# S5 recurrence and C powers moved from GpSimd to VectorE, S5 output steps placed between projections

## The chip, the core and the metric

One core of one Trainium2 chip runs one layer of a decoder for 256 prompt positions and 8 x 4 decode positions. The metric is the device time of one execution in microseconds. The engines are TensorE (PE; PEld is its weight load), VectorE (DVE), ScalarE (ACT), GpSimd (POOL) and SyncE (SP, which issues most loads). Each works through its own queue in order and waits on semaphores for the others.

## The reference, cut to what matters

The layer modulates a normalised input by conditioning vectors (adaLN), projects it to q, k, v, g, a_lr and u, runs gated linear attention (GLA, 4 heads) on the first five and an S5 state space group on u, mixes both through an output projection, and ends with a convolutional feed-forward part. The S5 part, to which the change belongs:

```python
lam_bar = jnp.exp(lam * dt)
b_bar = ((lam_bar - 1) / lam)[..., None] * bmat
bu = jnp.einsum('gpk,blgk->blgp', b_bar, uf.astype(jnp.complex64))
bu = bu.at[:, 0].add(lam_bar * h0)
_, h = lax.associative_scan(combine, (a, bu), axis=1)      # s_t = lam_bar s_(t-1) + bu_t
y = jnp.real(jnp.einsum('gkp,blgp->blgk', cmat, h)) + d_skip.astype(f32) * uf
```

There are 64 groups of 16 channels with 64 complex states each. All of it is float32.

## The kernel before

Activations lie transposed: features on partitions, the 32 decode and 256 prompt positions (288) as columns. A float32 product is made of three matmuls (mm3, L146 to L148): a weight tile `raw` of 128x1024 arrives by DMA, ScalarE rounds it to `wh` (L128), VectorE subtracts to get `wl` (L130, called the weight split), and wh is multiplied with the high and low part of the activation, wl with the high part. The results stand in three PSUM buffers `acc`, which ScalarE or VectorE must evict. Other matmuls: `ada` (L203, the adaLN projections, which run in the gaps of everything up to the feed-forward part), transposes against `ident`, and the small ones of GLA (`gl`) and S5 (`s`).

The input projection takes the 16 blocks of the contraction in K-groups of 2, 2 and 4 (column blocks acc evicted at L614 for the first group, by ScalarE, and at L616 and L618 for the others, by VectorE), and the last 8 of them in `proj2`, called for each of the 32 column blocks when it is wanted: u in 0 to 7, q in 8 to 11, k in 12 to 15, v in 16 to 23, g in 24 to 31. The S5 parameters are prepared beside the first groups: powers of A (`AP`, by `cmul`, L309 to L314), three powers of A times B (`pn`, L356 to L366) which TensorE transposes (L376), and C times the powers of A (`cA`, L394 to L400).

S5 works on blocks of four positions. Each of the eight steps f makes u of four pairs of groups, forms the states' inputs `st` (64 prompt columns and 8 decode columns for each of 2 x 32 rows) with TensorE (L714), and adds to every second column its neighbour times A^4 (`advance`, L684 and L687). Then the odd columns are carried through one after the other: 31 steps of four operations on 128x64 with A^8 (`a8`, L733 to L736), all on GpSimd, with `s5p` copied from the last one (L738). `s5_out(f)` advances the even columns of its f, and TensorE multiplies the states with cA (L895) and u with a local matrix (L891); ScalarE copies the result to `zt` (L898), TensorE transposes it (L901). The attention inside chunks follows a ladder of levels (VectorE L806 to L810, exponentials on ScalarE, TensorE L773 and L787). `dec_states` does the decode states of GLA with TensorE (L972, L984), on states loaded from `sgla` into two pairs of buffers in turn.

The order of the instructions on each engine is set when the program is built: a scheduler takes them by priority and by its own model of the times, with weight loads and splits raised by a fixed amount (AHEAD). `order_after` pins an instruction behind another of the same engine: the advance of an output step behind the eviction of the last g projection (`gadd`).

## Time and profile before

| what | us |
|---|---|
| median of 3 runs | 1459.36 |
| the three runs | 1458.64, 1459.36, 1469.23 |
| the profiled execution, its time | 1467.12 |
| its span (first to last instruction) | 1465.3 |
| TensorE busy in the span | 1408.3 |
| VectorE busy | 908.1 |
| ScalarE busy | 676.8 |
| GpSimd busy | 343.5 |
| mean granted TensorE clock | 0.983 |

The share of busy time is that of the whole span. The stages differ: the first 45 us prepare, the input projection runs to about 200 us, S5, q, k, v, g and attention lie between 200 and 430 us, the output projection follows, and from about 600 us on the feed-forward part fills TensorE. Busy time of TensorE counts a matmul at half clock in full, so the clock has to be read beside it.

### The profile page before, as it was taken

The page shows a single profiled execution, that of the slowest core. Times are in us where ns is not written, and L with a number is a line of the kernel's source. Part 1 is how long each engine was busy: PE and PEld are TensorE (multiplying, and loading weights), DVE is VectorE, ACT ScalarE, POOL GpSimd, SP SyncE. Part 2 cuts the span into 40 slices and gives each one's busy share as a digit, 9 for nine tenths or more (in the row PEclk, how much of TensorE's full clock was granted, in tenths as well). Part 3 has the DMA queues.
Part 4 walks back from the last instruction along what each step waited for, and adds up shares of the span by engine and source line. Part 5 has one row for each costly group of instructions (what it writes and reads, how often), then busy time and mean ns, then how long its engine had stood idle before and what let it go on. Part 6 is the DMA issues. An engine that isn't in the chain of part 4 may idle for free.

```text
span 1465.3 us, 29026 instructions
## 1 busy us (share of the span) xinstructions
PE 1408.3 (96%) x11546; PEld 1301.8 (89%) x11546; DVE 908.1 (62%) x1648; ACT 676.8 (46%) x1132; POOL 343.5 (23%) x616
## 2 busy tenths in 40 slices
...
GB/s 374 333 263 221 342 285 286 285 295 318 148 143 399 281 277 260 278 302 288 166 166 164 168 161 169 161 169 140 191 163 165 166 162 170 160 172 159 138 102 65
DMA packets 88727, 316.96 MB, mean 216 GB/s; under 512 B 10368, under 2 KB 10784, under 8 KB 88592
## 3 DMA queue, kind: packets, MB, share of 16 engines
...
q10 hardware_dynamic: 288, 0.59, 0.1%
...
## 4 chain that ended last, share of the span: by engine, by line
PE 72%; POOL 5%; DMA 1%; DVE 1%; issue 1%; ACT 0%; DVEq 0%; POOLq 0%; ACTq 0%
PE acc L146 22%; PE acc L147 22%; PE acc L148 22%; PE ada L203 2%; POOL st L736 1%; POOL q L733 1%; POOL q L734 1%; POOL st L735 1%; PE s L895 1%; DMA raw<-wadf 0%; PE s L891 0%; DMA o_glap<-S 0%; PE gl L972 0%; PE acc L1184 0%; PE acc L1185 0%
## 5 line engine op out<-in xcount | busy, mean ns | idle before, releaser
L128 ACT CAST wh<-raw 128x1024 fp32r<-128x1024 f32 (+1 forms) x376 | 385.6, 1030 | 565.7 <-PE acc L147 482.8
L130 DVE TENSOR_TENSOR wl<-raw,wh 128x1024 fp32r<-128x1024 f32 (+1 forms) x376 | 458.2, 1221 | 274.6 <-ACT wh L128 261.7
L146 PE MATMUL acc<-hh,wh 128*128 128x288 f32 x1360 | 402.8, 296 | 0.0
L147 PE MATMUL acc<-hl,wh 128*128 128x288 f32 x1360 | 401.1, 295 | 0.0
L148 PE MATMUL acc<-hh,wl 128*128 128x288 f32 x1360 | 399.9, 294 | 0.0
L146 PEld LDWEIGHTS acc<-hh,wh 128*128 128x128 f32 x1360 | 254.7, 187 | 3.6 <-ACT up L1197 1.1
L148 PEld LDWEIGHTS acc<-hh,wl 128*128 128x128 f32 x1360 | 256.1, 188 | 0.0
L147 PEld LDWEIGHTS acc<-hl,wh 128*128 128x128 f32 x1360 | 255.1, 188 | 0.8 <-issue 0.8
L1198 POOL COPY cvo<-up 128x16 f32<-128x16 f32 x88 | 99.6, 1131 | 582.1 <-ACT up L1196 582.1
L147 PE MATMUL acc<-ffhl,wh 128*128 128x288 f32 x704 | 208.1, 296 | 0.0
L148 PE MATMUL acc<-ffhl,wl 128*128 128x288 f32 x704 | 207.6, 295 | 0.0
L146 PE MATMUL acc<-ffhl,wh 128*128 128x288 f32 x704 | 207.0, 296 | 0.5 <-ACT ffhl L1228 0.2
L146 PE MATMUL acc<-h,wh 128*128 128x288 f32 x512 | 158.0, 309 | 2.0 <-DVE PG L618 1.2
L148 PE MATMUL acc<-h,wl 128*128 128x288 f32 x512 | 152.4, 300 | 3.1 <-DVE wl L130 3.1
L147 PE MATMUL acc<-h,wh 128*128 128x288 f32 x512 | 152.9, 299 | 0.9 <-DVE h L483 0.9
L147 PEld LDWEIGHTS acc<-ffhl,wh 128*128 128x128 f32 x704 | 132.7, 188 | 0.1
L146 PEld LDWEIGHTS acc<-ffhl,wh 128*128 128x128 f32 x704 | 131.9, 188 | 0.9 <-ACT ffhl L1228 0.5
L148 PEld LDWEIGHTS acc<-ffhl,wl 128*128 128x128 f32 x704 | 132.0, 188 | 0.0
L1062 DVE SCALAR_TENSOR_TENSOR x<-acc,mod,x 128x256 f32<-128x256 f32 x128 | 61.7, 482 | 101.9 <-PE acc L148 101.7
L146 PEld LDWEIGHTS acc<-h,wh 128*128 128x128 f32 x512 | 97.3, 190 | 24.9 <-issue 10.7
L203 PE MATMUL ada<-raw,cS 128*32 128x512 f32 (+1 forms) x832 | 101.5, 577 | 6.2 <-DMA raw<-wadf 3.7
L148 PEld LDWEIGHTS acc<-h,wl 128*128 128x128 f32 x512 | 96.9, 190 | 4.2 <-DVE wl L130 3.8
...
## 6 DMA issues: line engine op xcount, KB each, us to landing
...
raw<-wadf SPq DMA_DIRECT2D x128, 512.0 KB, 6.8
...
```

What stands on the lines that cost most here:

```text
L128: cast[0] = S.copy(wh, raw)
L130: V.tensor_sub(wl, raw, wh.bitcast(F32))
L146: T.matmul(ps, wh[:, ks], xh(k), start=first, stop=False)
L147: T.matmul(ps, wh[:, ks], xl(k), start=False, stop=False)
L148: tail[0] = T.matmul(ps, wl[:, ks], xh(k), start=False, stop=last).ins
L203: mms.append(lambda c=c, kc=kc_of(blk, j), raw=raw, c0=c0, first=first, last=last: T.matmul(ps[32 * c:32 * c + 32, 0:w], cS[:, kc, :], raw ...
L733: G.tensor_tensor(q1, prev, a8[:, 0], op=ALU.mult)
L734: G.tensor_tensor(q2, prevs, a8[:, 1], op=ALU.mult)
L735: G.tensor_tensor(cur, cur, q1, op=ALU.add)
L736: G.tensor_tensor(cur, cur, q2, op=ALU.add)
L1062: V.scalar_tensor_tensor(x2[:, m, ND:], ps[:, ND:], mod[:, vi, m, 0:1], x2[:, m, ND:], op0=ALU.mult, op1=ALU.add)
L1198: G.tensor_copy(cvo[:, m, 0:16].rearrange("p (b w) -> p b w", w=2), upd[:, :, 4:6])
```

## The change

Five things are changed. The C powers are computed by VectorE instead of GpSimd. The powers A^4, A^8, A^16, A^32 and A^64 (`apr`, `api`) are computed with the S5 parameters in place of `a4` and `a8`. All advances run on VectorE, and the serial recurrence on GpSimd is replaced by `scan` on VectorE: three levels up, three single columns, three levels down, 36 operations, once for the first half of the pair blocks (after f = 3) and once for the second (after f = 7). The output steps stand between the value and first gate projections (`fill(16)` to `fill(25)`), and the last six gate projections among the value transposes, the prompt state and the decode states. The pairs of buffers of the decode states change places.

```diff
@@ -391,13 +391,13 @@
             for n in range(4):
                 ar, ai = bc16(AP[:, n, 0]), bc16(AP[:, n, 1])
                 t1, t2 = tmp512(), tmp512()
-                G.tensor_tensor(t1, cc[:, 0], ar, op=ALU.mult)
-                G.tensor_tensor(t2, cin, ai, op=ALU.mult)
...
+                V.tensor_tensor(t1, cc[:, 0], ar, op=ALU.mult)
+                V.tensor_tensor(t2, cin, ai, op=ALU.mult)
...
@@ -513,6 +513,9 @@
                                      (cst, a["cst"][:, 0:C_ID])):
                         tc.keep_in_program_order(nc.sync.dma_start(dst, src))
 
+        apr = epb.tile([P, 5, 32], F32, name="apr")
+        api = epb.tile([P, 5, 2, 32], F32, name="api")
+
         def s5_rest(w1=w1, w2=w2, w3=w3):
             for o_, sc_ in ((sn, 1.0), (sh_, 0.5)):
                 sin_op = S.activation(o_, thr, AF.Sin, scale=sc_)
@@ -539,6 +542,15 @@
             V.tensor_mul(w2, w3, lam_i)
             V.tensor_sub(w1, w1, w2)
             V.tensor_mul(fi, w1, den)
+
+            for i in range(5):
+                if i == 0:
+                    V.tensor_copy(apr[:, 0], AP[:, 3, 0])
+                    V.tensor_copy(api[:, 0, 1], AP[:, 3, 1])
+                else:
+                    s_r, s_i = apr[:, i - 1], api[:, i - 1, 1]
+                    cmul(apr[:, i], api[:, i, 1], s_r, s_i, s_r, s_i, w1, w2)
+                V.tensor_scalar_mul(api[:, i, 0], api[:, i, 1], -1.0)
 
 
         h2 = [None]
@@ -664,27 +676,31 @@
             V.tensor_sub(l2, l2, l1)
             V.tensor_tensor_scan(cum[:, h], cst[:, C_RST:C_RST + NT], l2, 0.0, op0=ALU.mult, op1=ALU.add)
 
-
-        a4 = epb.tile([P, 2, 2, 32], F32, name="a4")
-        a8 = epb.tile([P, 2, 2, 32], F32, name="a8")
-        for t in (a4, a8):
-            if t is a4:
-                V.tensor_copy(t[:, 0, 0], AP[:, 3, 0])
-                V.tensor_copy(t[:, 1, 1], AP[:, 3, 1])
-            else:
-                cmul(t[:, 0, 0], t[:, 1, 1], AP[:, 3, 0], AP[:, 3, 1], AP[:, 3, 0], AP[:, 3, 1],
-                     t[:, 0, 1], t[:, 1, 0])
-            V.tensor_copy(t[:, 0, 1], t[:, 0, 0])
-            V.tensor_scalar_mul(t[:, 1, 0], t[:, 1, 1], -1.0)
-
-        def advance(eng, dst, src, srcs, fs, n, prev=None):
-            for w_, x in ((0, src), (1, srcs)):
-                q = t2k.tile([P, 512], F32, tag="t2k", name=nm("q"))[:, 0:8 * n].rearrange(
-                    "p (r a c) -> p r a c", r=2, a=4)
-                ins = eng.tensor_tensor(q, x, a4[:, w_, :, fs].unsqueeze(3).to_broadcast([P, 2, 4, n]), op=ALU.mult)
+        def advance(eng, fs, lev, c0, dist, n, prev=None):
+
+            na, back = fs.stop - fs.start, 1 << lev
+
+            def cols(rs, c):
+                return st[:, rs, fs, NB + 1 + c:NB + 2 + c + dist * (n - 1):dist]
+
+            dst = cols(slice(None), c0)
+            for w_, rs in ((0, slice(None)), (1, slice(None, None, -1))):
+                q = t2k.tile([P, 512], F32, tag="t2k", name=nm("q"))
+                q = q[:, 0:2 * na * n].rearrange("p (r a c) -> p r a c", r=2, a=na)
+                tr = (apr[:, lev, fs].unsqueeze(1).to_broadcast([P, 2, na]) if w_ == 0 else api[:, lev, :, fs])
+                ins = eng.tensor_tensor(q, cols(rs, c0 - back), tr.unsqueeze(3).to_broadcast([P, 2, na, n]), op=ALU.mult)
                 if prev is not None and w_ == 0:
                     order_after(ins.ins, prev)
                 eng.tensor_tensor(dst, dst, q, op=ALU.add)
+
+        def scan(eng, fs):
+
+            for lev in (1, 2, 3):
+                advance(eng, fs, lev, (2 << lev) - 1, 2 << lev, NC4 >> (lev + 1))
+            for c in range(31, NC4, 16):
+                advance(eng, fs, 4, c, 1, 1)
+            for lev in (3, 2, 1):
+                advance(eng, fs, lev, (3 << lev) - 1, 2 << lev, (NC4 >> (lev + 1)) - 1)
 
         ut = []
         for f in range(8):
@@ -715,25 +731,17 @@
                 S.copy(st[:, r, 4 * f:4 * f + 4, NB + 1:], pi[:, :, NB:])
                 S.copy(deci[:, r, 4 * f:4 * f + 4], pi[:, :, 0:NB])
             fs = slice(4 * f, 4 * f + 4)
-            advance(V if f == 7 else G, st[:, :, fs, NB + 2::2], st[:, :, fs, NB + 1::2], st[:, ::-1, fs, NB + 1::2], fs, 32)
+            advance(V, fs, 0, 1, 2, NC4 // 2)
+            if f % 4 == 3:
+                scan(V, slice(4 * f - 12, 4 * f + 4))
             step(ada_b, 1)
 
         dt1 = t2k.tile([P, 512], F32, tag="t2k", name="dt1").rearrange("p (r a b) -> p r a b", r=2, a=32)
         for w_, src in ((0, st[:, :, :, 0:NB]), (1, st[:, ::-1, :, 0:NB])):
             for r in range(2):
-                V.tensor_tensor(dt1[:, r], src[:, r], a4[:, w_, r].unsqueeze(2).to_broadcast([P, 32, NB]), op=ALU.mult)
+                V.tensor_tensor(dt1[:, r], src[:, r], (apr[:, 0] if w_ == 0 else api[:, 0, r]).unsqueeze(2).to_broadcast([P, 32, NB]), op=ALU.mult)
             V.tensor_add(deci, deci, dt1)
         G.dma_start(a["o_s5d"], deci)
-        for c in range(3, NC4, 2):
-            prev = st[:, :, :, NB + c - 1]
-            prevs = st[:, ::-1, :, NB + c - 1]
-            cur = st[:, :, :, NB + c + 1]
-            q1 = sml.tile([P, 2, 32], F32, tag="q1", bufs=1, name=nm("q1"))
-            q2 = sml.tile([P, 2, 32], F32, tag="q2", bufs=1, name=nm("q2"))
-            G.tensor_tensor(q1, prev, a8[:, 0], op=ALU.mult)
-            G.tensor_tensor(q2, prevs, a8[:, 1], op=ALU.mult)
-            G.tensor_tensor(cur, cur, q1, op=ALU.add)
-            G.tensor_tensor(cur, cur, q2, op=ALU.add)
         s5p = epb.tile([P, 2, 32], F32, name="s5p")
         G.tensor_copy(s5p, st[:, :, :, NCOL])
         G.dma_start(a["o_s5p"], s5p)
@@ -867,19 +875,13 @@
             S.copy(kFT[blk], pa)
 
 
-        for m in range(16, 24):
-            ps = proj2(m)
-            V.tensor_add(proj_dst(m), ps, proj_dst(m))
-            step(ada_b, 1)
-
         ybuf = []
 
         gadd = [None]
 
         def s5_out(f):
             fs = slice(4 * f, 4 * f + 4)
-            advance(G if f % 2 else V, st[:, :, fs, NB + 3::2], st[:, :, fs, NB + 2:NCOL:2], st[:, ::-1, fs, NB + 2:NCOL:2],
-                    fs, 31, None if f % 2 else gadd[0])
+            advance(V, fs, 0, 2, 2, NC4 // 2 - 1, gadd[0])
             zt = t2k.tile([P, 512], F32, tag="t2k", name=nm("zt"))
             ztv = zt[0:NCOL].rearrange("p (t a j k) -> p a j t k", t=4, a=4, j=2)
             pzs = [ps_s5()[0:NCOL, 0:256], ps_s5()[0:NCOL, 0:256]]
@@ -904,18 +906,20 @@
                           py[:, 0:4 * NCOL].rearrange("p (s c) -> p s c", s=4))
             ybuf.append(yb)
 
-        for f in range(8 + 4):
-            if f < 8:
-                ps = proj2(24 + f)
-                gadd[0] = V.tensor_add(proj_dst(24 + f), ps, proj_dst(24 + f)).ins
-                step(ada_b, 1)
-            if f >= 4:
-                s5_out(f - 4)
+        def fill(m):
+            ps = proj2(m)
+            gadd[0] = V.tensor_add(proj_dst(m), ps, proj_dst(m)).ins
+            step(ada_b, 1)
+
+        for i in range(10):
+            fill(16 + i)
+            if i >= 2:
+                s5_out(i - 2)
 
         vT = [slot("PQ", [P, 1024]), slot("PK", [P, 1024])]
         vTd = slot("cst", [P, DV])
         vT3 = slot("PT3", [P, 1024], F32R)
-        for blk in range(3):
+        def v_trans(blk):
             for hf in range(2):
                 pa = ps_gl()
                 n_ = P if blk < 2 else ND
@@ -932,6 +936,12 @@
                     S.copy(vT3[ND:2 * ND, cs_], pa[0:ND])
                     V.tensor_sub(vT3[2 * ND:3 * ND, cs_], pa[0:ND], vT3[0:ND, cs_].bitcast(F32))
 
+        v_trans(0)
+        fill(26)
+        v_trans(1)
+        fill(27)
+        v_trans(2)
+
 
         gp = slot("S11", [P, 4, DV])
         for h in range(H):
@@ -941,6 +951,7 @@
             S.copy(gp[:, h], pa)
         G.dma_start(a["o_glap"], gp)
 
+        fill(28)
 
         odz = t2k.tile([P, 512], F32, tag="t2k", name="odz")
         qbd = slot("PV0", [P, H, NB * (ND + NL)])
@@ -957,8 +968,8 @@
         for h in range(H):
             hs = slice(ND * h, ND * h + ND)
             T.matmul(po[hs], attd[hs], vTd[hs], start=True, stop=False)
-        for b2 in range(NB // 2):
-            if b2 % 2 == 0:
+        def dec_states(b2):
+            if b2 % 2:
                 s0 = [slot("S10", [P, 2, 2, DV]), slot("S11", [P, 2, 2, DV])]
             else:
                 mmh = slot("MM", [P, 2, 2, 2, DV])
@@ -988,6 +999,10 @@
                                            op0=ALU.mult, op1=ALU.add)
             for hf in range(2):
                 G.dma_start(a["o_glad"][b2, :, hf].rearrange("p (h b v) -> p h b v", h=2, b=2), s0[hf])
+        for b2 in range(NB // 2):
+            dec_states(b2)
+            if b2 < 3:
+                fill(29 + b2)
         S.copy(odz[:, 0:DV], po)
```

The built order shows where this moves instructions. First TensorE, near the end of what the first K-group of the input projection needs; `acc` are column blocks, `pn` the powers of A times B, `h` the activation. Before:

```order
L147 MATMUL acc_918<-h_196,wh_914 128x288
L148 MATMUL acc_918<-h_196,wl_916 128x288
L376 MATMUL s_105_648<-ident,pn_520 128x128 x4
L376 MATMUL s_106_655<-ident,pn_520 128x128 x4
L146 MATMUL acc_926<-h_196,wh_914 128x288
L147 MATMUL acc_926<-h_196,wh_914 128x288
L148 MATMUL acc_926<-h_196,wl_916 128x288
L146 MATMUL acc_926<-h_196,wh_914 128x288
L147 MATMUL acc_926<-h_196,wh_914 128x288
```

There the transposes stand behind the first column block of the second K-group (acc_918). Now:

```order
L147 MATMUL acc_574<-h_196,wh_533 128x288
L148 MATMUL acc_574<-h_196,wl_535 128x288
L376 MATMUL s_105_681<-ident,pn_553 128x128 x4
L376 MATMUL s_106_688<-ident,pn_553 128x128 x4
L376 MATMUL s_107_695<-ident,pn_553 128x128 x4
L146 MATMUL acc_582<-h_196,wh_533 128x288
L147 MATMUL acc_582<-h_196,wh_533 128x288
L148 MATMUL acc_582<-h_196,wl_535 128x288
L146 MATMUL acc_582<-h_196,wh_533 128x288
```

They stand behind acc_574, which is the block that was called acc_541 before, 18 column blocks earlier and inside the first K-group.

On VectorE, at the same place, with `wl` the weight splits, `PK` and `apr`, `api` the powers of A, `t` the products of 128x512. Before, from one split to behind the next:

```order
L130 TENSOR_TENSOR wl_573<-raw_569,wh_571 128x1024
L332 TENSOR_TENSOR s_s_102<-t_65_463,t_63_461 128x512
L452 SCALAR_TENSOR_TENSOR amul<-mod,vec 128x18
L357 TENSOR_TENSOR t_80_530<-s_s_102,AP 128x512
L362 TENSOR_TENSOR t_81_535<-s_s_102,AP 128x512
L464 TENSOR_TENSOR S_1_103<-S_1_103,amul 128x2x32
L471 SCALAR_TENSOR_TENSOR S_1_103<-S_1_103,amul,rst_186 128x256 x2
L360 TENSOR_TENSOR pn_520<-t_79_529,t_80_530 128x16x16 x2
L363 TENSOR_TENSOR t_82_536<-s_s_102,AP 128x512
L356 TENSOR_TENSOR t_85_557<-s_s_102,AP 128x512
L130 TENSOR_TENSOR wl_673<-raw_669,wh_671 128x1024
L366 TENSOR_TENSOR pn_520<-t_81_535,t_82_536 128x16x16 x2
```

Now, the last twelve rows ahead of the next split (wl_706; the one before it, wl_606, stands 48 rows ahead of wl_706):

```order
L311 TENSOR_TENSOR apr<-PK_114 128x32
L360 TENSOR_TENSOR pn_553<-t_99_649,t_100_650 128x16x16 x2
L312 TENSOR_TENSOR PK_114<-apr,api 128x32
L313 TENSOR_TENSOR PK_114<-api,apr 128x32
L363 TENSOR_TENSOR t_102_656<-s_s_102,AP 128x512
L394 TENSOR_TENSOR t_160_995<-s_s_102,AP 128x512
L314 TENSOR_TENSOR api<-PK_114 128x32
L366 TENSOR_TENSOR pn_553<-t_101_655,t_102_656 128x16x16 x2
L553 TENSOR_SCALAR api<-api 128x32
L395 TENSOR_TENSOR t_161_996<-s_s_102,AP 128x512
L398 TENSOR_TENSOR t_162_1000<-s_s_102,AP 128x512
L130 TENSOR_TENSOR wl_706<-raw_702,wh_704 128x1024
```

The chain of the powers of A times B, interleaved with the new powers of A and the first C power, stands between two splits, where before it was spread over several.

Last, the end of the second scan on VectorE: q<-st,apr 128x480 is its last level, dt and S the decode states, the rows of 248 the advance of output step 0, and the row behind these the first of the attention levels. Now:

```order
L691 TENSOR_TENSOR q_3138<-st,api 128x480
L742 TENSOR_TENSOR dt_3141<-st,apr 128x256 x2
L694 TENSOR_TENSOR st<-st,q_3135 128x2x16x15
L743 TENSOR_TENSOR S_372_2304<-S_372_2304,dt_3141 128x512
L694 TENSOR_TENSOR st<-st,q_3138 128x2x16x15
L691 TENSOR_TENSOR q_3953<-st,apr 128x248
L742 TENSOR_TENSOR dt_3141<-st,api 128x256 x2
L691 TENSOR_TENSOR q_3956<-st,api 128x248
L694 TENSOR_TENSOR st<-st,q_3953 128x2x4x31
L743 TENSOR_TENSOR S_372_2304<-S_372_2304,dt_3141 128x512
L694 TENSOR_TENSOR st<-st,q_3956 128x2x4x31
L814 TENSOR_TENSOR S_597_3523<-S_374_2326 128x4x4x32
```

And TensorE at the place that reads these states (L897 is L895 of before), with L730 the last state inputs and L781 the attention inside the smallest blocks:

```order
L730 MATMUL gl_3059<-UU_521_3057,PT_77_556 64x72 x8
L730 MATMUL gl_3070<-UU_521_3057,PT_78_557 64x72 x8
L893 MATMUL s_644_3961<-MM_1571,UU_396_2415 72x64
...
L781 MATMUL gl_3484<-PQ_295,PK_296 32x32 x8
L783 MATMUL gl_3484<-PQ_295,PK_296 32x32
L897 MATMUL s_643_3960<-cA,st 72x64 x2
L897 MATMUL s_644_3961<-cA,st 72x64 x2
L893 MATMUL s_643_3960<-MM_1571,UU_396_2415 72x64
```

The advance of output step 0 stands behind the scan, and TensorE has only small matmuls between the last state inputs and the first product with these states. Before, this place had adaLN matmuls and transposes of v, with the whole of the value projection and five gate projections ahead of it:

```order
L203 MATMUL ada_3915<-raw_4402,cS 32x512 x2
L203 MATMUL ada_3915<-raw_4400,cS 32x512 x2
L203 MATMUL ada_3915<-raw_4398,cS 32x512 x2
L203 MATMUL ada_3915<-raw_4396,cS 32x512 x2
L891 MATMUL s_729_4419<-MM_1538,UU_396_2396 72x64
L891 MATMUL s_730_4420<-MM_1538,UU_396_2396 72x64
L924 MATMUL gl_4870<-ident,PV_30_295 128x128 x2
L924 MATMUL gl_4876<-ident,PV_31_296 128x128 x4
L895 MATMUL s_729_4419<-cA,st 72x64 x2
L895 MATMUL s_730_4420<-cA,st 72x64 x2
```

The first product with the states comes later there relative to the projections.

8 lines of the change are left out of this document (4 added, 4 removed).

## The prediction

> **What bounds the kernel now.** The page comes first: TensorE is busy almost throughout. Line numbers are those of the kernel before.
>
> ```profile
> PE 1408.3 (96%) x11546; PEld 1301.8 (89%) x11546; DVE 908.1 (62%) x1648; ACT 676.8 (46%) x1132; POOL 343.5 (23%) x616
> PE 72%; POOL 5%; DMA 1%; DVE 1%; issue 1%; ACT 0%; DVEq 0%; POOLq 0%; ACTq 0%
> ```
>
> The second line is the chain of waits: 5% of the span, some 73 us, lies on GpSimd. Then the stretches of time (stretch and its length; busy time and instructions of PE, PEld, DVE, ACT, POOL; granted TensorE clock; DMA share; GB/s), first one of the feed-forward part, then those around the S5 recurrence.
>
> ```profile
> 680.00:690.00 10.00, 10.00 (x77) 10.00 (x77) 5.90 (x11) 4.09 (x9) 2.97 (x8) 1.00 0.91 319
> 355.00:360.00 5.00, 2.82 (x26) 1.10 (x18) 0.39 (x1) 2.14 (x4) 4.53 (x15) 1.00 1.03 401
> 360.00:365.00 5.00, 1.12 (x17) 1.15 (x18) 3.14 (x5) 0.00 (x0) 4.37 (x9) 0.51 0.91 351
> 365.00:370.00 5.00, 5.00 (x48) 4.88 (x45) 0.54 (x1) 2.25 (x5) 2.42 (x4) 0.50 0.27 92
> 395.00:400.00 5.00, 2.66 (x58) 2.32 (x60) 0.68 (x1) 2.37 (x4) 3.16 (x5) 1.00 0.50 172
> 400.00:420.00 20.00, 17.89 (x185) 14.80 (x178) 7.75 (x16) 7.59 (x20) 3.75 (x6) 0.53 0.15 54
> ```
>
> The first row is the full rate, 77 matmuls in 10 us or 0.13 us each. Nothing after about 600 us is touched by the change and TensorE is full there, so the time is settled by how early TensorE gets through the first 430 us. The waits of TensorE from 280 to 600 us (total, times, longest) name the holes:
>
> ```profile
> PE s L895 <- POOL s5p L738: 6.1, 1, 6.1
> PE ada L203 <- DMA raw<-wadf: 3.7, 1, 3.7
> PE gl L972 <- DMA S<-sgla: 2.3, 1, 2.3
> ```
>
> An earlier hole lies where GpSimd computes the C powers:
>
> ```profile
> 110.00:115.00 5.00, 3.57 (x25) 3.39 (x26) 5.00 (x7) 0.70 (x1) 2.93 (x4) 1.00 1.00 375
> 115.00:120.00 5.00, 3.13 (x17) 2.40 (x20) 4.51 (x5) 1.05 (x1) 4.92 (x3) 0.77 0.45 152
> 130.00:135.00 5.00, 2.90 (x143) 2.77 (x138) 4.82 (x8) 0.00 (x0) 1.57 (x2) 0.98 0.25 99
> 155.00:160.00 5.00, 2.54 (x18) 1.29 (x20) 1.89 (x5) 0.92 (x3) 0.00 (x0) 0.87 1.02 380
> ```
>
> **What is removed.** (a) The wait of 6.1 us for the serial recurrence, and the half clock behind it. TensorE idles 2.2 us in 355-360 and 3.9 in 360-365 and loses half of its 1.1 + 5.0 busy us to the clock: 9.1 us. (b) S5 output steps 4 to 7 run in 395-420 with no large matmul beside them: 2.3 us idle, then 2.1 idle and 0.47 x 17.89 = 8.4 lost to the clock: 12.8 us. With projections between the steps, as before has them in 372-395, the rate should be full. Together **-22 us**.
>
> (c) GpSimd's 24 products of 128x512 run beside VectorE at 100-131 us. VectorE's rows then (start, duration):
>
> ```profile
> 106.03 2.19 DVE L473 SCALAR_TENSOR_TENSOR h<-S,mod,h 128x256 fp32r<-128x256 f32 x2
> 112.39 4.81 DVE L130 TENSOR_TENSOR wl<-raw,wh 128x1024 fp32r<-128x1024 f32 x1
> ```
>
> Undisturbed, as the rows below show, the weight split takes 1.22 us. On VectorE the 24 products cost 0.60 us each, 14.4 us. In the new order 21 of them stand in the input projection's second K-group, with 9 splits (1.14 each), 28 evictions (0.37) and some 5 us of small steps: 38 to 40 us. That group takes 48 us before (from 63.2, just ahead of the first row below, to 111.8, the second). So VectorE becomes its limit, and it is still **-8 us**.
>
> ```profile
> 64.04 1.04 PE L376 MATMUL s<-ident,pn 128*128 128x128 f32 x8
> 111.79 0.40 PE L147 MATMUL acc<-h,wh 128*128 128x288 f32 x1 [0.87 <-DVE h L483]
> ```
>
> From 112 to 160 us the rows above show about 8 us of idle TensorE (3.3 in 110-120, 2.1, 2.5) and three half-clock pieces of about 1.7 us loss each, 13 us in all. Only the first 5 are plainly GpSimd's; the rest (a load, an issue gap) may go because TensorE will be late there. I take **-8 us**, between -5 and -13.
>
> **What is added: an early stall.** The order quoted with the change has 12 transposes of the B powers (L376) directly behind acc_574, 18 column blocks earlier than before. They wait for the third power on VectorE, and VectorE now runs that whole chain, with four more levels of A powers between its steps, without a weight split in it. The prices come from before's rows there:
>
> ```profile
> 43.41 1.22 DVE L130 TENSOR_TENSOR wl<-raw,wh 128x1024 fp32r<-128x1024 f32 x1
> 44.55 0.69 DVE L332 TENSOR_TENSOR s_s<-t,t 128x512 f32<-128x512 f32 x1
> 45.27 0.69 DVE L357 TENSOR_TENSOR t<-s_s,AP 128x512 f32<-128x512 f32 x1
> 45.88 0.69 DVE L362 TENSOR_TENSOR t<-s_s,AP 128x512 f32<-128x512 f32 x1
> 47.41 0.76 DVE L360 TENSOR_TENSOR pn<-t,t 128x256 f32<-128x256 f32 x2
> 48.20 0.69 DVE L363 TENSOR_TENSOR t<-s_s,AP 128x512 f32<-128x512 f32 x1
> 35.05 0.17 DVE L673 COPY a<-AP 128x32 f32<-128x32 f32 x1
> 35.14 0.18 DVE L310 TENSOR_TENSOR a<-AP 128x32 f32<-128x32 f32 x1
> 44.03 0.29 PE L148 MATMUL acc<-h,wl 128*128 128x288 f32 x1
> ```
>
> By starts: the split 1.14, a 512 product 0.60, a 256 one 0.39, a small one 0.10. From the split at 43.41 up to the awaited row stand 1 split, 11 x 0.60, 8 x 0.39, 20 x 0.10 and 1 us of others: 13.9 us, so the transposes start near 57.7. TensorE is there at 44.2 (last row). It idles 13.5 us, and a half-clock piece behind it costs 1.7. The 38 transposes that are then already done (0.10 each, by the row at 64.04) pay for evictions that ScalarE now does late. **+15 us**; nothing else stands ahead of the wait on TensorE, so only group 1 can give any of it back, 9 us if VectorE's head start made it TensorE's again (about 31 us: 192 matmuls, three groups of adaLN matmuls, 30 transposes).
>
> **A stall at the second scan.** TensorE's first state matmul of S5 output step 0 needs its advance, and on VectorE that stands behind the advance of f = 7, the whole scan of the second half and the decode states, although its data are of the first half. Between TensorE and that wait lie only 1.5 us of small matmuls. The rows for VectorE's prices:
>
> ```profile
> 380.43 0.46 DVE L910 TENSOR_TENSOR PG<-acc,PG 128x288 f32<-128x288 f32 x1
> 380.80 0.73 DVE L684 TENSOR_TENSOR q<-st,a 128x248 f32<-128x248 f32 x2
> 381.47 0.40 DVE L687 TENSOR_TENSOR st<-st,q 128x248 f32<-128x248 f32 x1
> 381.79 1.21 DVE L130 TENSOR_TENSOR wl<-raw,wh 128x1024 fp32r<-128x1024 f32 x1
> 382.93 0.82 DVE L687 TENSOR_TENSOR st<-st,q 128x248 f32<-128x248 f32 x1
> 383.80 0.48 PE L895 MATMUL s<-cA,st 64*72 64x64 f32 x8
> L694 DVE TENSOR_TENSOR us<-acc,UU x8: 661/688/778, 204.9 to 252.8; 128x288 f32<-128x288 f32 x8
> L618 DVE TENSOR_TENSOR UU<-acc,UU x16: 442/449/459, 64.6 to 142.4; 128x288 f32<-128x288 f32 x16
> ```
>
> A product of 248 costs 0.335 (380.80 to 381.47 for two), of 512 0.60: 0.08 us and 1.02 ns an element. A scan of half the blocks is 36 operations on 7168 elements: 10 us. Its columns lie 16 bytes and more apart. The last two rows (min, median, max in ns) are the same size, L694 reading at steps of 16 bytes, L618 in sequence: 239 ns more on 288 elements, 0.83 ns each. Level 0 of the advance, at steps of 8 bytes, shows no such price. At 0.83 the scan costs 6 us more. I take L694's price, as it has the same step, and keep none as the lower end: 16 us, with 1.3 + 1.3 for the two advances, 2.5 for the decode states and 0.5 for a mask copy 21.6, less 1.5 of cover: 20 us idle, and 2 of half clock as in 365-370. **+22 us** (16 to 26). The first scan lies beside two q-projections and costs at most 3.
>
> The Trainium skill (Vector Engine (DVE) Microarchitecture Reference, section Measured stream behaviour on trn2) speaks against such scans: single words stepped far apart cost up to 2.5 ns each instead of 1.05. The rows agree in kind, at 1.85 ns for steps of 16 bytes. By the page's 2.5 the second scan would be an estimated 20.6 us and the sum 4 us higher.
>
> **Smaller terms.** The attention levels (L806 to L810) stood beside projections before; now their 20 dense VectorE products (12 x 0.60 and 8 of 576 elements at 0.67) and some 9 us of other steps stand against about 16 us of TensorE work: 5 us, less 2 that it lost at 310-320 (its row for 315-320 is busy for 3.33 of 5): **+3**, 0 to 8.
>
> ```profile
> 315.00:320.00 5.00, 3.33 (x143) 3.08 (x142) 5.00 (x8) 0.96 (x2) 4.76 (x7) 1.00 0.90 320
> 376.07 0.42 PE L901 MATMUL tr<-ident,zt 72*128 72x72 f32 x4
> 375.28 0.64 ACT L898 COPY zt<-s 72x256 f32<-72x256 f32 x2 [1.16 <-PE s L895]
> ```
>
> Each output step now follows its projection's eviction on VectorE, with a weight split between its two sums. The rows from 380.43 to 383.80 are that chain: 3.4 us, some 3.0 without GpSimd beside it. Before, adaLN and gla matmuls cover it; now steps 3, 5 and 7 have 0.3 to 1.3 us of cover and wait about 2.3, 1.7 and 2.7, steps 2 and 4 about 0.5 each. The copies of zt delay the transposes behind them by 0.7 (375.28 to 376.07), uncovered in four steps. **+11**, 0 to 15. A later TensorE no longer waits for the load at 585 us: **-3**. Where the decode states now wait for the slot MM, two projections and two adaLN groups cover the load: 0.
>
> **Sum.** -22 - 8 - 8 + 15 + 22 + 3 + 11 - 3 = +10 us. The profiled span is 1465.3 (1467.1 with what lies around it), so the same execution would have 1475. The median is 1459.4, 8 us below it, and I put the same difference on it: **1470 us**.
>
> **Rivals.** *The stalls stay short* (faster). VectorE, free while TensorE waits, makes group 1 TensorE's again: 15 becomes 6. The scan has no price for steps: 16. All 13 us at 112-160 go, attention costs nothing, the rounds 3. Sum 6 - 8 - 13 - 22 + 16 + 3 - 3 = -21: 1438 us. For it speaks level 0 at the plain price; against it the order. Chance 0.22.
>
> *Only the scan and the rounds are cheaper* (no change): -6 and -8 on the sum, 1456 us. Chance 0.18.
>
> *The clock stays down* (slower). Between scan 2 and the last output step TensorE is busy for some 60% of the time, less than the 89% at which 400-420 held 0.53. If half of the S5 and projection work of that stretch, about 60 us, ran at 0.5, 13 to 15 us more: 1484. It decides if the stretches there read under 0.8. Against it: 380-395 holds 1.00 with the same mixture. The Trainium skill (TensorE: Matmul & The Clock Gate, Part 1) has half rate after one idle window of about 3.4 us; by that only the two long stalls are paid for, as summed. Chance 0.17.
>
> That the recurrence did not gate TensorE is excluded by the 6.1 us row. My forecast has 0.43, with 1460 to 1481 as its own range.
>
> **Numbers.** 1% is 14.6 us, about what can be told from no change: faster is below 1444.8, slower above 1474. Faster: most of the first rival and a little of the second, 0.23. Slower: the third rival and two fifths of the forecast's own range, 0.33. The rest 0.44. The range reaches from the first rival's 1438, a little cut, to beyond the third's 1484: 1440 to 1488.
>
> **What would show it.** Right: TensorE idle for about 13 us near 44 to 58, ended by pn on VectorE; another 15 to 21 us near 300, ended by st; no row with s5p; L395-L400 on VectorE in 80-125; waits of 2 to 3 us ahead of L895's successor in three rounds; VectorE's products of 480 and 512 in the scan at about 1 us rather than 0.6. Wrong: either stall under 5 us, or a half clock over the whole stage.

## The result, and the profile after

The changed kernel takes 1509.03 us (median of four executions, 1505.02 to 1514.07) against 1461.51 for the kernel before: a ratio of 1.032, with a 95% interval of 1.0265 to 1.037. It is slower by some 46 us where 1470 us, no change within the bounds, was forecast. The profiled execution took 1507.93 us with a span of 1506.0 and a mean granted clock of 0.972.

Busy times and the chain of waits by engine, from the page of the changed kernel:

```profile
PE 1409.5 (94%) x11546; PEld 1303.7 (87%) x11546; DVE 951.3 (63%) x1807; ACT 677.5 (45%) x1132; POOL 209.6 (14%) x424
PE 72%; DVE 2%; DMA 2%; issue 1%; ACT 1%; DVEq 0%; ACTq 0%; POOLq 0%
```

TensorE does the same work (1409.5 us busy, 1408.3 before), and the 5% of the chain that lay on GpSimd are gone. Its waits over the whole span (total, times, longest) show what came in place (a wait of 14 us at L442 stands in both kernels and is left out):

```profile
PE s L897 <- DVE st L694: 28.8, 6, 22.1
PE s L376 <- DVE pn L360: 13.2, 1, 13.2
PE gl L781 <- DVE S L818: 5.5, 2, 2.9
PE tr L903 <- ACT zt L900: 5.0, 4, 2.3
PE ada L203 <- DMA raw<-wadf: 4.2, 2, 3.5
```

The two long waits are the two stalls of the forecast, 13.2 us for the B powers early on and 22.1 at the first state matmul of output step 0. The wait on s5p is not there. The kernel before, in the 20 us in which the early stall falls, with the columns as in the prediction:

```profile
40.00:60.00 20.00, 19.13 (x161) 17.46 (x164) 19.34 (x39) 17.23 (x39) 0.00 (x0) 1.00 0.92 345
```

The stretches of the changed kernel, first the early stall and then the second scan with what follows it:

```profile
40.00:50.00 10.00, 4.30 (x33) 4.00 (x31) 10.00 (x29) 6.16 (x13) 0.00 (x0) 0.82 0.86 344
50.00:60.00 10.00, 2.50 (x11) 2.20 (x12) 10.00 (x36) 1.33 (x5) 0.00 (x0) 0.50 0.01 2
...
310.00:320.00 10.00, 1.80 (x96) 1.54 (x92) 8.69 (x16) 0.92 (x4) 0.77 (x1) 0.80 0.69 253
320.00:330.00 10.00, 0.00 (x0) 0.00 (x0) 9.66 (x29) 0.00 (x0) 0.83 (x2) 0.50 0.01 3
330.00:340.00 10.00, 3.86 (x49) 3.70 (x50) 6.24 (x13) 2.31 (x4) 0.54 (x1) 0.50 0.06 26
340.00:350.00 10.00, 7.00 (x189) 6.33 (x188) 5.86 (x13) 6.26 (x10) 0.00 (x0) 0.83 0.01 2
350.00:360.00 10.00, 6.28 (x236) 5.96 (x239) 9.88 (x20) 3.00 (x4) 0.00 (x0) 0.51 0.16 56
```

VectorE is full in both stalls, and from 310 to 360 TensorE is busy for 19 of 50 us, mostly at half clock. Rows of VectorE in the second scan (start, duration):

```profile
313.04 1.06 DVE L691 TENSOR_TENSOR q<-st,apr 128x512 f32<-128x512 f32 x1
314.01 1.05 DVE L691 TENSOR_TENSOR q<-st,api 128x512 f32<-128x512 f32 x1
```

By starts a product of 512 at steps of 16 bytes takes 0.97 us, or 1.9 ns an element, against 0.60 us in sequence. The Trainium skill (Vector Engine (DVE) Microarchitecture Reference, section Measured stream behaviour on trn2) has 1.71 to 2.51 ns an element where single words are stepped, by which operands step and how far. The trace agrees in kind: 1.9 ns lies in that range.

To compare stages, the table adds up, over stretches of 5 us, the idle time of TensorE and what it lost to the clock (busy time times one minus the granted clock). "First u" is where the first S5 step's u is formed; for the changed kernel that is the first start in this row of its groups (min, median, max in ns, then first and last start):

```profile
L710 DVE TENSOR_TENSOR us<-acc,UU x8: 646/686/735, 211.2 to 282.0; 128x288 f32<-128x288 f32 x8
```

| kernel (profiled execution, us) | ratio | first u | 40 to 250: idle + clock | 250 to 480: idle + clock | span |
|---|---|---|---|---|---|
| before | 1 | 204.9 | 9.3 + 4.3 | 12.5 + 12.4 | 1465.3 |
| changed | 1.032 | 211.2 | 18.2 + 2.9 | 42.9 + 13.6 | 1506.0 |
| e1_powers_late | 1.021 | 195.5 | 4.7 + 0.0 | 41.8 + 13.6 | 1488.6 |
| e2_scan2_later | 1.032 | 213.9 | 19.4 + 4.3 | 36.9 + 23.6 | 1512.2 |
| e3_out_later | 1.026 | 210.1 | 18.3 + 2.1 | 34.6 + 11.9 | 1496.1 |
| e4_cpow_pool | 1.034 | 217.6 | 21.2 + 6.8 | 42.6 + 13.9 | 1512.2 |
| e5_scan_alone | 1.000 | 197.8 | 7.7 + 1.4 | 15.3 + 9.8 | 1461.4 |
| e6_cpow_alone | 1.000 | 198.7 | 6.7 + 1.0 | 11.0 + 12.3 | 1460.8 |
| e7_interleave_alone | 1.018 | 197.1 | 6.0 + 1.4 | 42.1 + 8.9 | 1488.4 |
| e8_hybrid | 1.0035 | 196.3 | 5.9 + 0.0 | 22.4 + 7.9 | 1467.7 |
| e9_old_places | 0.999 | 195.4 | 4.6 + 0.0 | 14.9 + 10.8 | 1459.0 |
| e10_old_places_early_powers | 1.0095 | 211.3 | 18.3 + 3.8 | 16.5 + 9.6 | 1475.8 |
| e11_warm (matmuls put into the stall) | 1.030 | 211.6 | 18.2 + 3.0 | 26.5 + 14.2 | 1509.5 |
| e12_spread | 1.004 | 195.5 | 4.5 + 0.0 | 16.9 + 16.1 | 1467.8 |
| e13_pin | 1.030 | 211.8 | 19.5 + 2.0 | 44.2 + 14.8 | 1509.5 |
| e14_odd_pool | 0.997 | 196.1 | 4.9 + 0.0 | 17.0 + 7.7 | 1460.1 |
| e15_scratch | 1.022 | 198.1 | 6.7 + 1.7 | 42.3 + 14.9 | 1493.9 |

Of the 40.7 us between the first two spans, 7.5 lie in the early part and 31.6 in the S5 and attention stage (21.1 less 13.6, 56.5 less 24.9). The other kernels of the table are told below.

### The profile page after: what moved, and what is told of

Its sections match the earlier page's. It is cut to its first block, busy times and chain, and to the rows that moved or that the text cites. A ratio compares the mean times of both kernels' runs of the same rounds, so it can differ in the third digit from the quotient of the medians.

```text
span 1506.0 us, 28991 instructions
## 1 busy us (share of the span) xinstructions
PE 1409.5 (94%) x11546; PEld 1303.7 (87%) x11546; DVE 951.3 (63%) x1807; ACT 677.5 (45%) x1132; POOL 209.6 (14%) x424
## 4 chain that ended last, share of the span: by engine, by line
PE 72%; DVE 2%; DMA 2%; issue 1%; ACT 1%; DVEq 0%; ACTq 0%; POOLq 0%
PE acc L146 22%; PE acc L148 22%; PE acc L147 22%; PE ada L203 3%; PE s L897 1%; DMA MM<-sgla 1%; DMA raw<-wadf 1%; DVE wl L130 1%; DMA o_glad<-MM 0%; PE s L893 0%; PE acc L1199 0%; PE acc L1200 0%; PE tr L903 0%; PE acc L1203 0%; PE gl L983 0%
## 5 line engine op out<-in xcount | busy, mean ns | idle before, releaser
L130 DVE TENSOR_TENSOR wl<-raw,wh 128x1024 fp32r<-128x1024 f32 (+1 forms) x376 | 450.9, 1202 | 291.0 <-ACT wh L128 278.4
L146 PE MATMUL acc<-h,wh 128*128 128x288 f32 x512 | 160.9, 315 | 2.1 <-DVE PK L630 1.6
L147 PE MATMUL acc<-h,wh 128*128 128x288 f32 x512 | 154.2, 302 | 0.0
```

Source lines behind the costliest of these rows:

```text
L130: V.tensor_sub(wl, raw, wh.bitcast(F32))
L146: T.matmul(ps, wh[:, ks], xh(k), start=first, stop=False)
L147: T.matmul(ps, wh[:, ks], xl(k), start=False, stop=False)
```

## The experiments

The first four undo one part of the changed kernel each.

**e1_powers_late.** The five powers are formed where a4 and a8 were, with a scratch tile of their own.

```diff
             V.tensor_mul(fi, w1, den)
-            for i in range(5):
...
-                    cmul(apr[:, i], api[:, i, 1], s_r, s_i, s_r, s_i, w1, w2)
...
+        pw = sml.tile([P, 2, 32], F32, tag="q1", bufs=1, name="pw")
+        for i in range(5):
...
+                cmul(apr[:, i], api[:, i, 1], s_r, s_i, s_r, s_i, pw[:, 0], pw[:, 1])
```

> One part undone: the five levels of powers of A (apr, api) are computed just ahead of the first S5 step, where a4 and a8 stood before, instead of among the S5 parameters; all else as in the changed kernel (1509 us, against 1461 before). In the built order the transposes of the B powers (L376) then stand behind the third block of the second K-group again. Theory A (the early stall of 13 us and the lag of 16 to 20 us behind it come from the chain of powers on VectorE that the new powers lengthened and gathered): the stall goes, 12 to 20 us faster, 1489 to 1497 us. Rival C (the early loss comes from the C powers on VectorE): within 5 us of 1509.

Measured: 1495.42 us, ratio 1.021 (1.018 to 1.024). The early wait is gone and a third of the loss with it; the 22.1 us of wait at step 0 stay. In the program the edit moves two things, the place of the powers and their scratch. In the built order only the scratch differs much: the scheduler has the powers start at 34.3 to 58.9 us here and at 34.7 to 59.8 in the changed kernel. The last sum of the powers, in the changed kernel and then in e1:

```profile
59.02 0.18 DVE L314 TENSOR_TENSOR api<-PK 128x32 f32<-128x32 f32 x1
```

```profile
57.48 0.20 DVE L314 TENSOR_TENSOR api<-pw 128x32 f32<-128x32 f32 x1
```

So where powers are called late, in this run and in e9, e12 and e14, they are late in the program alone; what these runs change in fact is the scratch.

**e2_scan2_later.** The second scan stands behind output step 1, whose data are of the first half.

```diff
-            if f % 4 == 3:
-                scan(V, slice(4 * f - 12, 4 * f + 4))
+            if f == 3:
+                scan(V, slice(0, 16))
...
+            if i == 3:
+                scan(V, slice(16, 32))
```

> One part moved: the scan of the second half of the blocks is issued behind S5 output step 1 instead of ahead of the decode states; all else as in the changed kernel. Theory A (TensorE waits 22 us because the advance of step 0 stands behind a scan whose data it does not need): the wait at step 0 goes to under 6 us, a smaller one comes ahead of step 2, which stands behind the scan now; 8 to 18 us faster, 1491 to 1501. Rival B (VectorE's work as a whole is the limit of this stage, wherever it stands): 1505 to 1513.

Measured: 1511.03 us, ratio 1.032 (1.029 to 1.0345), so my expectation fell and the rival's held. TensorE's waits from 180 to 600 us:

```profile
PE s L894 <- DVE st L694: 15.5, 7, 5.2
PE tr L900 <- ACT zt L897: 5.2, 4, 2.4
PE gl L778 <- DVE S L815: 5.1, 2, 2.9
PE gl L792 <- DVE PT L784: 4.4, 1, 4.4
```

Output step 0 now starts at 319.8 us and no wait is longer than 5.2, but the sum of idle time and clock from 250 to 480 is 60.5 us, where it was 56.5: the idle time fell by 6.0 and the loss to the clock rose by 10.0. Taking the long wait away alone gains nothing. The likely reason, which this run doesn't show by itself, is that VectorE has scan, advances and attention to do in that stretch whatever their order, and that TensorE has too little other work meanwhile.

**e3_out_later.** The output steps start four value or gate groups later.

```diff
-        for i in range(10):
+        for i in range(14):
             fill(16 + i)
-            if i >= 2:
-                s5_out(i - 2)
+            if i >= 6:
+                s5_out(i - 6)
```

> One part changed: the S5 output steps come four projections later, so that fill(16) to fill(21) stand ahead of step 0 and gate projections 26 to 29 are taken from between the later steps; all else as in the changed kernel. In the built order some 90 large matmuls more stand beside the second scan. Theory A (the scan is expensive only because nothing stands beside it): the wait at step 0 falls from 22 to 4 to 10 us, the half clock around it shrinks, 10 to 22 us faster, 1487 to 1499. Rival B (VectorE's total work is the limit): 1505 to 1513, the wait reappears later.

Measured: 1502.88 us, ratio 1.026 (1.023 to 1.029). The wait at step 0 fell from 22.1 to 12.4 us. The direction was right, the gain (8 us by the ratio) smaller than I expected.

**e4_cpow_pool.** The C powers are GpSimd's again (V to G in their six lines).

> One part undone: the C powers are computed by GpSimd again; all else as in the changed kernel. Theory A: the early stall of 13 us stays, and the disturbance of VectorE at 105 to 135 us comes back: 3 to 10 us slower, 1512 to 1519. Rival C (the C powers on VectorE cause the early loss): 10 to 18 us faster, 1491 to 1499.

Measured: 1513.34 us, ratio 1.034 (1.031 to 1.0365). That is 3 us over the changed kernel, and the intervals overlap. The early stall is 13.2 us as in the changed kernel, so the C powers on VectorE are not its cause.

The next four start from the kernel before and do one part alone.

**e5_scan_alone.** The kernel before with the recurrence as scans on VectorE; output steps, their advances and the C powers stay as they were.

```diff
             advance(V if f == 7 else G, fs, 0, 1, 2, NC4 // 2)
+            if f % 4 == 3:
+                scan(V, slice(4 * f - 12, 4 * f + 4))
...
-        for c in range(3, NC4, 2):
...
-            G.tensor_tensor(cur, cur, q2, op=ALU.add)
```

> One part alone: the kernel before (1462 us), with the serial recurrence on GpSimd replaced by the two scans on VectorE (their powers computed late, where a4 and a8 stood); C powers, advances and the places of the output steps as before, so that all value projections and five gate projections stand ahead of output step 0. Theory A (a scan costs time only where TensorE has nothing beside it): the wait of 6 us at step 0 goes, 3 to 10 us faster, 1452 to 1459. Rival B (VectorE has no room for some 36 us more between 260 and 370 us, wherever it stands): 5 to 25 us slower, 1467 to 1487, with new waits of TensorE on VectorE in the attention.

Measured: 1464.47 us, ratio 1.000 (0.998 to 1.002), between the two expectations. The waits from 180 to 600 us:

```profile
PE acc L148 <- DVE wl L130: 3.9, 3, 1.7
PE s L903 <- DVE st L695: 2.3, 2, 2.0
PE s L899 <- ACT zt L906: 2.0, 1, 2.0
PE s L903 <- POOL st L695: 1.8, 1, 1.8
```

The output steps start at 346.4 us. In the profile of the kernel before they start at 363.9, but that profile is 7 us later at the first u already. In e6, which keeps the serial recurrence and whose first u is within 1 us of this one, they start at 357.8, after a wait of 2.6 us on s5p. So the scan brings them some 11 us forward, and nothing came of it at the end: the loss from 250 to 480 is 25.1 us, before 24.9, in e6 23.3.

**e6_cpow_alone.** The kernel before with the C powers on VectorE (G to V in their six lines).

> One part alone: the kernel before with the C powers on VectorE. From the run with the powers of A moved back, whose first S5 step came at 195.5 us against 204.9 before, both theories expect 6 to 10 us faster, 1452 to 1456; if VectorE's second K-group only becomes its own limit, 1459 to 1463.

Measured: 1462.92 us, ratio 1.000 (0.9985 to 1.002): a miss, as 8 to 12 us less were expected. Its profile is 6 us ahead at the first u, but those of e5 and e7, which leave the C powers on GpSimd, are 7 and 8 ahead. The profiled execution of the kernel before is the one that is late there; at 1467.1 us it lies 3 us and more above the medians of that kernel in these comparisons (1461.5 to 1464.3).

**e7_interleave_alone.** The kernel before with the new places of output steps, value and gate groups, and with the decode states' buffers in the changed order; the recurrence stays serial on GpSimd.

```diff
-        for m in range(16, 24):
...
-        for f in range(8 + 4):
...
+        for i in range(10):
+            fill(16 + i)
+            if i >= 2:
+                s5_out(i - 2)
```

> One part alone: the kernel before with the new places of the output steps and last gate projections; the recurrence stays serial on GpSimd, the C powers too. Theory A: what the new places take away is cover, whatever computes the recurrence: ten projections, some 40 us, stand behind step 0 instead of ahead of it, so the wait at step 0 grows from 6 to 30 to 45 us and the total is 10 to 30 us slower, 1472 to 1492; that near to the changed kernel the placement would be a main cause. Rival B (the scan's work on VectorE is the cause): within 8 us of before, 1454 to 1470.

Measured: 1490.68 us, ratio 1.018 (1.015 to 1.020), as the first theory had it, though the wait at step 0 is 18.5 us and not 30 to 45. Its waits from 180 to 600 us:

```profile
PE s L907 <- DVE st L696: 20.0, 3, 18.5
PE gl L791 <- DVE S L828: 9.2, 4, 4.3
PE gl L805 <- DVE S L828: 7.3, 1, 7.3
```

The first row is the recurrence, late for step 0 now; the other two are the attention's levels, uncovered.

**e8_hybrid.** From the kernel before: the C powers and one level of the scan on VectorE, the other 15 steps serial on GpSimd, and output step 0 behind group 24 in place of 28, so that each of the eight output steps has a group ahead of it.

> A version meant to beat both: the kernel before with the C powers on VectorE; one level of the scan up and down on VectorE, so that GpSimd's serial part has 15 steps instead of 31; output step 0 one projection earlier, so that all output steps have a projection. Theory A: GpSimd ends some 25 us earlier, the waits and half clock at 355 to 370 (9 us) and most of those at 395 to 421 (13 us) go, with 8 from the C powers: 15 to 30 us faster, 1433 to 1448. Rival B (VectorE has no room for 16 us more there): 1450 to 1462.

Measured: 1469.51 us, ratio 1.0035 (1.002 to 1.005): slower than either theory. A wait of TensorE and a row of VectorE tell why:

```profile
PE gl L794 <- DVE S L831: 14.4, 3, 6.7
```

```profile
324.40 1.00 DVE L692 TENSOR_TENSOR q<-st,apr 128x480 f32<-128x480 f32 x1 [6.29 <-POOL st L755]
```

The scan's level down stands in VectorE's order ahead of the next product of the attention (L830, at 327.2 us) and waits for the serial part on GpSimd. The attention, and TensorE with its longest wait of 6.7 us, wait behind it.

The theory by then was that two prices add: something of the early powers, and the large matmuls that the new places take away from beside VectorE's scan and attention. Three kernels with the old places test it.

**e9_old_places.** The changed kernel with the powers as in e1 and groups 16 to 28 ahead of output step 0, groups 29, 30 and 31 behind the steps 0, 1 and 2, and nothing kept back (the order is written here as loops).

```diff
-        for i in range(10):
-            fill(16 + i)
-            if i >= 2:
-                s5_out(i - 2)
+        for m in range(16, 29):
+            fill(m)
+        for f in range(8):
+            s5_out(f)
+            if f < 3:
+                fill(29 + f)
...
-        fill(26)
...
-        fill(27)
...
-        fill(28)
...
-            if b2 < 3:
-                fill(29 + b2)
```

> The changed kernel with its recurrence as scans and its C powers on VectorE, but with the powers of the step formed where the two old tables were, and with value groups 16 to 28 ahead of the first output step, as the kernel before had them; nothing is kept back for between the attention's small products. Theory A (what the changed kernel loses is the large matmuls that no longer stand beside the second scan, the attention's level chain and the early phase products): 1455 to 1464 us, ratio 0.994 to 1.002 (the scan alone and the C powers alone measured 1.000 each), with the wait of TensorE on st at the first output step under 3 us and half clock under 45 us. Theory B (VectorE's load together, scans, advances and C powers, is the price wherever the matmuls stand): 1475 to 1490, ratio over 1.008, with waits of TensorE on VectorE of more than 15 us in the S5 stage.

Measured: 1460.52 us, ratio 0.999 (0.997 to 1.000). Two stretches of e1 and then four of e9:

```profile
300.00:320.00 20.00, 1.79 (x28) 1.82 (x30) 17.58 (x44) 0.00 (x0) 1.37 (x3) 0.50 0.11 44
320.00:340.00 20.00, 12.28 (x292) 11.25 (x291) 14.19 (x26) 9.74 (x14) 0.00 (x0) 0.59 0.10 30
```

```profile
300.00:320.00 20.00, 20.00 (x155) 16.19 (x157) 19.66 (x43) 4.95 (x5) 2.11 (x2) 1.00 0.86 291
320.00:340.00 20.00, 18.22 (x140) 13.87 (x132) 15.63 (x26) 7.09 (x8) 0.54 (x1) 1.00 0.96 359
340.00:360.00 20.00, 13.81 (x380) 12.46 (x376) 16.64 (x34) 12.14 (x16) 0.00 (x0) 0.74 0.49 193
360.00:380.00 20.00, 18.50 (x206) 15.33 (x207) 6.26 (x13) 9.77 (x21) 0.00 (x0) 0.66 0.07 20
```

VectorE has the second scan in hand in these first 20 us of both (17.58 and 19.66 busy). In e9 it does so in pieces between weight splits, and TensorE is full beside it; in e1 TensorE stands. Between the two kernels lie 0.022 in the ratio, 32 us. As e9 keeps the changed order of the decode states' buffers, that part of the change costs nothing that shows here.

**e10_old_places_early_powers.** The same with the powers early and their scratch in w1 and w2.

> The same, but with the five powers of the step formed early, where the change has them. Theory A (the early wait on the phase product and the place of the value projections are two prices that add): ratio 1.008 to 1.014 (1475 to 1483 us), being the 1.011 by which the late powers bettered the changed kernel; the wait of about 13 us on pn at 44 to 58 us is back and no other. Theory B (the early wait's loss is taken up by slack in the S5 stage when the places are the old ones): 0.999 to 1.005, within 5 us of the kernel with late powers.

Measured: 1476.31 us, ratio 1.0095 (1.007 to 1.012). The early wait is back at 13.2 us. The prices add: 0.0106 for the powers with their scratch (e10 less e9) and 0.022 for the places (e1 less e9) on 0.999 make 1.0316, and the changed kernel has 1.0318.

**e12_spread.** As e9, with the last three groups spread by twos among the output steps.

```diff
-            if f < 3:
-                fill(29 + f)
+            if f in (0, 2, 4):
+                fill(29 + f // 2)
```

> The kernel with late powers and old places, with the last three value groups spread by twos (group 29 after output step 0, group 30 after steps 1 and 2, group 31 after steps 3 and 4) in place of one after each of the first three steps. If what is left to gain are the half clocks and waits in the row of the last output steps: 3 to 8 us below the kernel with old places, 1448 to 1458. If the steps' pace is set by VectorE's and ScalarE's hand-overs within a step and not by what stands between two: within 2 us of it.

Measured: 1469.41 us, ratio 1.004 (1.002 to 1.006), 8 us slower than e9 and a miss for both. Its loss to the clock from 250 to 480 is 16.1 us, in e9 10.8; why two steps in a row are worse here was not tried further.

**e11_warm.** The changed kernel with 150 matmuls of 128x288 put into the long stall, to keep TensorE busy there.

```diff
+            if f == 0:
+                wo = ps_acc()
+                for i in range(150):
+                    wm = T.matmul(wo, h2t[:, 0, i % 8, 0:128], h2t[:, 0, i % 8, 0:288], start=i == 0, stop=i == 149)
...
```

> The changed kernel with 150 matmuls of 128x288 whose result nothing reads (some 0.133 us each, 20 us) in the 22 us in which TensorE waits for the second scan, behind the attention's first small products and ahead of output step 0, so that TensorE isn't idle there; the same order otherwise but for two places of 48 small products. Theory A (the half clock behind the stall comes from the idle, and is paid by what TensorE does until the clock is back): the stretch of half clock from 316 to 343 us is gone, output step 0 and the value group behind it run at the full clock, and the time is 3 to 6 us lower, ratio 1.0275 to 1.030. Theory B (the small products themselves bring the half clock, as in the row at 400 us of the kernel before, or ScalarE and VectorE set the pace of step 0 anyway): half clock again within 5 us of step 0's start, and a ratio within 0.002 of 1.032.

Measured: 1507.87 us, ratio 1.030 (1.028 to 1.033). Four stretches and two rows of TensorE:

```profile
320.00:330.00 10.00, 10.00 (x77) 10.00 (x76) 9.66 (x29) 0.00 (x0) 0.84 (x2) 1.00 0.01 3
```

```profile
333.50:336.90 3.40, 1.79 (x44) 1.69 (x44) 1.10 (x3) 0.37 (x1) 0.54 (x1) 0.99 0.19 77
336.90:340.30 3.40, 0.00 (x0) 0.00 (x0) 1.26 (x2) 0.00 (x0) 0.00 (x0) 0.50 0.02 5
...
343.70:347.10 3.40, 3.40 (x16) 3.36 (x15) 0.00 (x0) 0.17 (x1) 0.00 (x0) 0.50 0.00 0
```

```profile
334.74 0.48 PE L909 MATMUL s<-cA,st 64*72 64x64 f32 x8 [2.37 <-DVE st L695]
...
341.78 0.74 PE L915 MATMUL tr<-ident,zt 72*128 72x72 f32 x4 [5.24 <-ACT zt L912]
```

The clock stays up through the stall, step 0's products run at full clock, and then TensorE waits 5.2 us for the copy of zt, and the value group behind runs at half clock all the same. The second theory held on both counts: half clock again 2 us after step 0's start, and a ratio lower by 0.0014, which is 2 us and less than its interval. But the loss to the clock from 250 to 480 stayed as it was (14.2 us, 13.6 in the changed kernel), so what a full clock over the whole stage would be worth is not shown.

**e14_odd_pool.** As e9, with the advance of the odd output steps on GpSimd, as before.

```diff
-            advance(V, fs, 0, 2, 2, NC4 // 2 - 1, gadd[0])
+            advance(G if f % 2 else V, fs, 0, 2, 2, NC4 // 2 - 1, None if f % 2 else gadd[0])
```

> The kernel with late powers and old places, with the advance of the odd output steps on GpSimd again, as the kernel before has it; the scans, the other advances and the C powers stay on VectorE. If VectorE's load in the row of output steps is what is left to gain: 3 to 8 us below the kernel with old places, ratio 0.994 to 0.997. If GpSimd's slower products make the odd steps wait, or the pace there is ScalarE's: ratio 0.997 to 1.002.

Measured: 1459.96 us, ratio 0.997 (0.996 to 0.998). This is the fastest of all and 4 us below the kernel before; from e9 its interval doesn't tell it apart, so it doesn't decide between its two expectations.

**e13_pin.** What remained open was how the early powers cost 15 us. My step in the prediction was that TensorE's transposes stand too early. Here they are issued 14 column blocks later and pinned, with the powers left early.

```diff
+            for _ in range(7):
+                yield
             for hf in range(2):
...
-                            T.transpose(pp[:, i], src[:, 64 * (w0 + i):64 * (w0 + i) + P], ident)
+                            tp = T.transpose(pp[:, i], src[:, 64 * (w0 + i):64 * (w0 + i) + P], ident)
+                            if w0 == 0 and i == 0:
+                                order_after(tp.ins, tail[0])
...
-            for _ in range(8):
+            for _ in range(1):
```

> The changed kernel with its early powers, but the transposes of the B powers issued 14 column blocks later in the program (seven of the eight idle steps behind the C powers put ahead of them) and the first of them pinned behind the column block issued before it, so that they stand where they stand with late powers. Theory A (what the early powers cost is the place that the transposes take on TensorE because of them): the wait of 13 us on pn is gone, and the ratio is within 0.003 of the kernel with late powers: 1.018 to 1.024 (1490 to 1499 us), first S5 step near 196 us. Theory B (the 20 small steps and the chain ahead of the splits on VectorE cost it by themselves, TensorE starving for weights or evictions in place of pn): ratio over 1.027, first S5 step later than 205 us.

Measured: 1509.72 us, ratio 1.030 (1.028 to 1.033): my step fell, since the place of the transposes is not what costs. The stall stays, and has moved to a large matmul. A wait of TensorE, a row of VectorE and one of ScalarE:

```profile
PE acc L146 <- ACT PK L630: 15.5, 1, 15.5
```

```profile
59.06 0.19 DVE L314 TENSOR_TENSOR api<-PK 128x32 f32<-128x32 f32 x1
```

```profile
59.34 1.01 ACT L630 ACTIVATE PK<-acc 128x288 f32<-128x288 f32 x3 [11.78 <-DVE api L314]
```

ScalarE's evictions of the k blocks into PK wait for the last of the powers. The scratch rows w1 and w2 are part of a table that lies in the buffer PK, until the k blocks (12 to 15) take that buffer over; the powers keep it in use until 59 us. With three acc buffers full TensorE can't go on, and whatever stands next in its order waits. In the changed kernel the first eviction into PK starts at 59.3 us too, and the transposes at 57.5: two waits of nearly one length, of which the profile names the first.

**e15_scratch.** The changed kernel with that scratch alone moved.

```diff
+            pw = sml.tile([P, 2, 32], F32, tag="q1", bufs=1, name="pw")
             for i in range(5):
...
-                    cmul(apr[:, i], api[:, i, 1], s_r, s_i, s_r, s_i, w1, w2)
+                    cmul(apr[:, i], api[:, i, 1], s_r, s_i, s_r, s_i, pw[:, 0], pw[:, 1])
```

> The changed kernel with the early powers where the change has them, but their two scratch rows in a tile of their own in place of w1 and w2, which lie in the buffer PK that the column blocks 12 to 15 are evicted into. Nothing else is edited. Theory A (the early stall is ScalarE's evictions into PK waiting for the last of the powers, TensorE standing behind them with its three buffers full): the wait of 13 us is gone with the powers still early, TensorE is busy for over 9 us in 40 to 50 and in 50 to 60, the first S5 step is near 196 us and the ratio 1.018 to 1.024 (1490 to 1499 us). Theory B (VectorE's early work as such starves TensorE): first S5 step later than 205 us and a ratio over 1.027.

Measured: 1495.01 us, ratio 1.022 (1.019 to 1.025), e1's within the interval. The stretches of the early part, and ScalarE's first eviction into PK:

```profile
40.00:50.00 10.00, 8.85 (x83) 7.52 (x82) 9.88 (x31) 8.96 (x21) 0.00 (x0) 1.00 0.94 363
50.00:60.00 10.00, 10.00 (x78) 9.67 (x80) 10.00 (x25) 7.86 (x18) 0.00 (x0) 1.00 0.93 342
```

```profile
44.72 1.02 ACT L627 ACTIVATE PK<-acc 128x288 f32<-128x288 f32 x3 [0.16 <-DVE t L331]
```

VectorE is as full as in the changed kernel, the powers are as early, and TensorE runs through (8.85 in the first stretch is a little under the 9 expected). The cause of the early stall is the shared buffer, since nothing else was edited. The built order follows the edit, though: the transposes start at 64.8 us, not 57.5, and four weight splits stand on VectorE from 49 to 61 us, where the changed kernel has none between 43.6 and 62.9. e13 shows that the blocked evictions alone are enough for the stall; that the scheduler drew the transposes forward because of them is likely, but not shown.

## Why the prediction was wrong

The forecast was 10 us over its base; 46 were measured. Term by term, with the price from pairs of kernels (difference of the ratios times 1464 us):

- **Early stall, +15.** Its size was right (13.2 us of wait against 13.5; 14 us by the scratch alone, 15.5 from e9 to e10), its reason wrong. "They wait for the third power on VectorE" is what the row of the profile says, but a run with the transposes later waited as long. The step that failed is "nothing else stands ahead of the wait on TensorE": a second wait stood right behind it, for full acc buffers whose evictions had no buffer to go to. That the size fits is partly luck, as the last power, which frees that buffer, stands near the end of the same chain on VectorE (59.0 us, the transposes start at 57.5; the 13.9 us of the sum, from 43.41, end at 57.3 and not at 57.7). The diff shows the sharing, in the last two arguments of cmul; I costed the 20 steps at 0.10 us and not what they hold.
- **(c), -8 and -8.** The C powers are worth nothing alone (e6, 1.000) and about 3 us in the changed kernel (e4). I had read the losses at 112 to 160 us out of one profile, which is 6 to 9.5 us later at the first u than every kernel without the early stall, those with the C powers on GpSimd among them; why it is, these runs don't settle. The first rival's whole gain at this place, -13, fell with it. This term was off by 13 to 16 us.
- **(a) and (b), -22.** This is the step that failed in the S5 stage. For (a), the wait on s5p went, and yet the loss from 250 to 480 us is 25.1 us in e5 and 25.7 in e9, 24.9 before. The 6.1 us were the last wait in a row of waits, and 2.6 in the profile of e6. Output steps that start sooner meet the attention, whose small products wait for VectorE (in e9 once for 5.0 us, the first row below), and half clock comes with that (0.74 and 0.66 from 340 to 380 in e9). For (b), "the rate should be full" with projections between the steps. The changed kernel has them there, and its clock still falls (the other two rows), so that the loss to the clock from 250 to 480 is 13.6 us against 12.4 before.

```profile
PE gl L783 <- DVE S L820: 5.0, 1, 5.0
```

```profile
380.00:390.00 10.00, 9.54 (x88) 8.07 (x84) 2.12 (x6) 2.14 (x4) 0.00 (x0) 0.66 0.16 54
...
420.00:430.00 10.00, 5.70 (x56) 5.52 (x57) 5.46 (x11) 4.71 (x12) 1.58 (x3) 0.59 0.72 254
```

- **Second-scan stall, +22, attention, +3, rounds, +11.** 36 in all. The wait of 22.1 for 20 idle, the price of the stepped reads, VectorE as the engine waited for and waits of up to 2.7 us in the rounds came as foretold. The sizes were too small: in idle time and clock the changed kernel loses 26.6 us from 310 to 340 (the stall, step 0 and its copy of zt), 11.0 from 340 to 360 (the attention's levels and step 1) and 16.8 from 360 to 440 (the other six steps), 54 together. Net of what the kernel before loses from 250 to 480 the stage costs 31.6 where +14 was forecast (36 less 22). One can put the 18 us between them down to the added terms or to the -22; e5 and e9, which gained nothing from the wait that went, speak for the latter.
- **Load at 585, -3.** It did not come. TensorE has no idle time from 480 to 610 us in the changed kernel, but the wait on the same load stands behind 610, 4.2 us.
- **The base.** 8 us were taken off for the distance between profiled execution and median. The medians of the kernel before in the later comparisons, 1461.5 to 1464.3, make that 3 to 6. Also, 1475 is the span with 10 us added, while the 8 us are the distance of the median from 1467.1; 1470 is the median of 1459.4 with 10 us added.

Together, (c) with 13 to 16, the S5 stage with 18 and the load with 3 make up the 36 us by which the forecast was too low; what the base was off by is within what these numbers leave open.

Of the rivals, "the clock stays down" was nearest. The sum leaves some 3 us of loss to the clock in this stage (12.4 before, less 11.5 in (a) and (b), and 2 more), the rival 16 to 18, and 13.6 were measured. By its own sign it held in part: the stretches read 0.50 to 0.83 from 310 to 360 and 0.66 and 0.59 in the two above, but 0.98 and 1.00 in others between them. Whether this loss has a price of its own is open, as e11 kept the clock up through the stall alone. What decides is the cover: large matmuls that stand beside VectorE's scan and beside the attention's levels (e9 against e1, 32 us), and the new places hold them back for the output steps, which alone they can't repay.
